# A hybrid encoder layer on one core: one pair's scan a step ahead, some transfers on POOL's queue, values turned later, and a decay product on ScalarE

## The chip, the cores and the metric

The kernel runs on one core of a Trainium2 chip. A core has TensorE (PE, matmuls and 128x128 transposes into PSUM), VectorE (DVE), ScalarE (ACT), GpSimd (POOL) and SyncE (SP, which here only issues transfers). Each engine works through its own list of instructions in order, and waits at an instruction until the data that it needs is there. The metric is the device time of one execution in microseconds (us); three executions are timed, and their median counts.

## The reference

One layer of an encoder trunk over 1024 tokens of width 1024, in float32. Each of three sub-layers is normalised before and after, and added to the residual stream.

```python
h = _rms_norm(x, g_mix_pre[l])
proj = h @ w_in[l]
aq, ak, av, dqkv, dgate, dalpha, dbeta = jnp.split(proj, IN_SPLITS, axis=-1)
...
attn_o = _window_attention(aq, ak, av, attn_sink[l])            # 8 heads of 64, 2 key heads, +-128 tokens
dn_o = _gated_deltanet(dqkv, dgate, dalpha, dbeta, conv_w[l], ...)
mix = jnp.concatenate([attn_o, dn_o], axis=-1) @ w_out[l]
x = x + _rms_norm(mix, g_mix_post[l])
c = _memory_cross_attention(...)                                # 256 memory tokens, 4 heads of 256
x = x + _rms_norm(c, g_cross_post[l])
f = _swiglu(...)                                                # width 2816
x = x + _rms_norm(f, g_ffn_post[l])
```

The gated DeltaNet has four heads, each scanned forwards and backwards over chunks. Within a chunk a triangular system is solved; over the chunks runs

```python
def step(state, inp):
    qg_i, kg_i, u_i, w_i, qk_i, gl_i = inp
    v_new = u_i - jnp.einsum('bhck,bhkv->bhcv', w_i, state)
    o_i = jnp.einsum('bhck,bhkv->bhcv', qg_i, state) + jnp.einsum('bhij,bhjv->bhiv', qk_i, v_new)
    state = state * gl_i[..., None, None] + jnp.einsum('bhck,bhcv->bhkv', kg_i, v_new)
    return state, o_i
```

## The kernel before

Products in full precision are made of three matmuls: each operand is split into its value in the type float32r and the rest (`split`, L99: an ACT copy and a VectorE or POOL subtraction), and high x high, low x high and high x low are summed in PSUM. `gemm_b` (L258) does this over the eight tiles of 128 of the width, 48 matmuls for one projection tile of 128 columns over two halves of 512 tokens.

The kernel hands its instructions to a planner, which keeps the program's order as priority, simulates times, and from these fixes each engine's order, SP's transfers among them. The lists of letters in L36 to L38 give the program's order in three stages:

- `ORDER_1`: projections of the DeltaNet's heads (D), their preparation (P), and the base inverses of two heads together (B, `base_inverse`, L505). A base inverse is a long chain of small VectorE products (L536, L538); that of the second pair of heads still runs while the next stage works.
- `ORDER_2`: `levels` (L, L548) builds the inverses of 128-token chunks from their 32x32 blocks. It fetches blocks with twenty small transfers (L553) into D5, D6, Z0, Z1, of which there is one set, and stores each head's result with four transfers to `d_pz` (L612). `gate_proj` (G), `attn_proj` (A, queries for 0 to 3, keys for 4) and `value_proj` (V) are projections; W stands for two windows of the softmax attention (`next_windows`, L683; a window's scores wait for its queries `qs`, L627).
- `ORDER_3`: M normalises the memory, `s01` makes one step of both scans, W two windows, K one tile of memory keys, V half of the memory values (whose weights are loaded by `load_w`, L127).

`attn_proj` (L723) turns queries and keys by rotary angles: `sn` and `rop` are the projection times sine and cosine (L731, L732), four transfers turn `sn` by 32 partitions into `rot` (L736), and the sum is split into `qhi` and `qlo` and stored to DRAM (L741). `sn`, `rot`, `qhi`, `qlo` and `rop` have two buffers each; `value_proj` (L743) copies its projection to `vT` (L748), which takes a buffer of the tag of `sn`, and PE turns it at once (L751) into `ptv`, split into `vhl`, which the windows use.

`scan(g)` (L773) is a generator for pair `g` of heads, two directions each, so that every tile holds four 128x128 blocks. There are eight steps. A step loads `kv` (k turned, v, k, q; two loads of 512 KB) and `pz` (two of 256 KB) on SP (L795, L796), and yields four times: after R, after the new values (L817), after the new state (L828), after the output. `scan_step` (L943) takes four such pieces, alternating between the pairs it is given. From step 4 on the output is normalised and, one step later, turned, gated and stored by `late` (L867); a ninth call of a scan runs the last `late`. In steps 1 to 3 the output is

```python
nc.vector.tensor_tensor(o, pq, eg(0), ALU.mult)   # L840: query part from PSUM times its decay
nc.vector.tensor_tensor(o, o, po, ALU.add)        # L841
```

and is first read at step 4 or later. The scan's tiles (pool `t3`, L771) take the space of the normalised input `hT` and of the projections' tiles; a tile waits until what lay there has been read.

## Time and profile before

| what | value |
|---|---|
| median of three executions | 1552.57 us (1552.0 to 1556.1) |
| profiled execution, own time | 1553.31 us |
| its span (first to last instruction) | 1551.3 us |
| PE busy | 1493.7 us |
| VectorE busy | 1064.2 us |
| ACT busy | 713.3 us |
| POOL busy | 301.1 us |
| moved by the DMA engines | 247.16 MB, 159 GB/s on average |

The profile is of one execution. Times in it count from the start of its span. "Busy" is the time in which an engine had an instruction in work; a matmul's start and end overlap with its neighbours', so the distance from start to start says more than a duration. The granted clock is the share of TensorE's full rate that the throttle let through. A row of the timeline has the start, the duration, the engine and line, the operation, the tile written and the tiles read, and in brackets how long the engine had stood idle before it and what ended that. "SPq" rows are issues of transfers on SP.

### The profile page before, as it was taken

Reading aid. Unit: us, or ns where it says so; the run is one execution under the profiler, and the core shown is the slowest. Engines: PE = TensorE matmul, PEld = TensorE weight load, DVE = VectorE, ACT = ScalarE, POOL = GpSimd, SP = SyncE. Lnnn points to the kernel's source line nnn. Section 1 sums busy time; section 2 is a strip of 40 time slices with the busy share of each in tenths; the row PEclk is TensorE's granted clock in tenths of the full one; section 3 lists DMA queues with packets and bytes.
Section 4 is the critical chain, followed back from the end, with each engine's and each line's share of the span. In section 5 each row is a group of like instructions: output and inputs, shape, how many; then the busy total and the mean of one; then the engine's idle time right before and its main releaser. Section 6 shows DMA issues by size and latency. Waiting matters only on the chain.

```text
span 1551.3 us, 20930 instructions
## 1 busy us (share of the span) xinstructions
PE 1493.7 (96%) x7451; PEld 1255.3 (81%) x7451; DVE 1064.2 (69%) x1762; ACT 713.3 (46%) x1377; POOL 301.1 (19%) x297
## 2 busy tenths in 40 slices
PE   6999999988999999999999999999999999999998
PEld 5888888777899877888888787888888888888786
DVE  6877898766898765543446377786867654696676
ACT  5665552246556864464335564332323332454532
POOL 2000110000003201163202231443534333000010
PEclk9999999998999999999999999999999999999999
DMA  6244456768988584354223164344433334753355
GB/s 207 73 134 122 133 151 164 214 176 249 328 277 253 169 289 139 127 191 149 69 68 123 55 228 137 116 136 129 142 122 124 102 102 146 288 190 102 109 175 165
DMA packets 267366, 247.16 MB, mean 159 GB/s; under 512 B 39016, under 2 KB 204797, under 8 KB 267261
## 3 DMA queue, kind: packets, MB, share of 16 engines
q1 hardware_dynamic: 267261, 245.82, 50.7%
q8 instruction: 59, 0.97, 0.3%
q14 instruction: 46, 0.38, 0.1%
HBM read 173.65 MB, written 69.50 MB: 157 GB/s over the span
## 4 chain that ended last, share of the span: by engine, by line
PE 77%; DVE 9%; DMA 8%; SPq 2%; ACT 2%; issue 2%; POOL 0%; DVEq 0%; ACTq 0%; POOLq 0%
PE pmg L1020 10%; PE pg L263 10%; PE pE L1208 8%; PE pA L1208 7%; PE pD L1208 7%; PE pcq L263 6%; PE pdX L1398 6%; PE pdA L1398 4%; PE pB L1208 4%; PE psc L787 3%; PE pdX L1491 2%; PE pdD L1398 2%; PE pcs L1112 1%; PE pco L1138 1%; DMA wraw<-in_w_ckv_dram 1%
## 5 line engine op out<-in xcount | busy, mean ns | idle before, releaser
L102 ACT CAST whi<-wraw 128x1024 fp32r<-128x1024 f32 x108 | 113.4, 1050 | 172.9 <-PE pg L263 36.0
L103 DVE TENSOR_TENSOR wlo<-wraw,whi 128x1024 fp32r<-128x1024 f32 x78 | 95.4, 1224 | 69.5 <-ACT whi L102 64.9
L263 PE MATMUL pg<-hhi,whi 128*128 128x512 f32 x352 | 140.5, 400 | 2.0 <-DVE rop L732 2.0
L263 PE MATMUL pg<-hlo,whi 128*128 128x512 f32 x352 | 139.9, 398 | 0.0
L263 PE MATMUL pg<-hhi,wlo 128*128 128x512 f32 x352 | 139.6, 397 | 0.0
L1020 PE MATMUL pmg<-whi,b 128*128 128x512 f32 x384 | 118.3, 394 | 0.4 <-ACT b L102 0.4
L1208 PE MATMUL pA<-s,whi 128*128 128x512 f32 x352 | 109.4, 392 | 1.0 <-ACT m L1225 1.0
L103 POOL TENSOR_TENSOR wlo<-wraw,whi 128x1024 fp32r<-128x1024 f32 x30 | 73.1, 2437 | 142.2 <-ACT whi L102 142.1
L1020 PEld LDWEIGHTS pmg<-whi,b 128*128 128x128 f32 x384 | 71.3, 188 | 15.1 <-ACT b L102 1.3
L263 PEld LDWEIGHTS pg<-hhi,whi 128*128 128x128 f32 x352 | 67.1, 191 | 15.7 <-DVE rop L732 2.4
L263 PEld LDWEIGHTS pg<-hlo,whi 128*128 128x128 f32 x352 | 67.2, 191 | 13.1
L263 PEld LDWEIGHTS pg<-hhi,wlo 128*128 128x128 f32 x352 | 67.0, 190 | 13.1
L1398 PE MATMUL pdX<-dhl,whi 128*128 128x512 f32 x264 | 76.1, 390 | 1.5 <-DVE zv L1453 0.8
L1208 PEld LDWEIGHTS pA<-s,whi 128*128 128x128 f32 x352 | 65.5, 188 | 14.8 <-ACT m L1225 1.5
L1020 PE MATMUL pmg<-wlo,b 128*128 128x512 f32 x192 | 71.5, 392 | 0.0
L1208 PE MATMUL pA<-s,wlo 128*128 128x512 f32 x176 | 68.6, 391 | 0.0
L102 ACT CAST whi<-araw 128x1024 fp32r<-128x1024 f32 (+1 forms) x36 | 35.4, 982 | 71.0 <-PE pdX L1398 27.6
L103 DVE TENSOR_TENSOR wlo<-araw,whi 128x1024 fp32r<-128x1024 f32 (+1 forms) x36 | 40.8, 1133 | 39.5 <-ACT whi L102 39.4
L1285 POOL TENSOR_TENSOR act<-act,up 128x512 f32<-128x512 f32 x33 | 50.1, 1518 | 88.8 <-DVE up L1284 47.3
L288 DVE SCALAR_TENSOR_TENSOR acc<-cp,cols,acc 128x1024 f32<-128x1024 f32 x48 | 61.4, 1281 | 1.5 <-ACT acc L286 0.8
L1398 PEld LDWEIGHTS pdX<-dhl,whi 128*128 128x128 f32 x264 | 49.3, 188 | 12.7 <-issue 1.1
L1258 DVE TENSOR_TENSOR sr<-sr,wraw 128x512 f32<-128x512 f32 x22 | 36.6, 1663 | 28.2 <-POOL sr L1257 28.2
(410 smaller groups left out, 3969.1 us busy)
## 6 DMA issues: line engine op xcount, KB each, us to landing
wraw<-in_w_gate_up_dram SPq DMA_DIRECT2D x52, 512.0 KB, 3.9
kv<-d_kv SPq DMA_DIRECT2D x32, 512.0 KB, 6.7
wraw<-in_w_in_dram SPq DMA_DIRECT2D x22, 512.0 KB, 5.0
b<-in_w_down_dram SPq DMA_DIRECT2D x20, 512.0 KB, 6.9
araw<-d_as SPq DMA_DIRECT2D x20, 512.0 KB, 3.7
pz<-d_pz SPq DMA_DIRECT2D x32, 256.0 KB, 7.1
wraw<-in_w_ckv_dram SPq DMA_DIRECT2D x16, 512.0 KB, 6.4
wraw<-in_w_out_dram SPq DMA_DIRECT2D x16, 512.0 KB, 4.1
```

Source lines behind the costliest of these rows:

```text
L102: nc.scalar.copy(hi, src)
L103: (eng or nc.vector).tensor_tensor(lo, src, f32(hi), ALU.subtract)
L263: nc.tensor.matmul(p_, w[:, k, :], ah[a][:, k, :], start=(k == 0 and i == 0), stop=(k == nk - 1 and i == 2))
L288: nc.vector.scalar_tensor_tensor(acc, cp[:, t:t + S], taps[t], acc, ALU.mult, ALU.add)
L787: nc.tensor.matmul(out[:, d, h, :], lt[:, d, h, :], rt[:, d, h, :], start=True, stop=True)
L1020: nc.tensor.matmul(pp[t], act[a][:, k, tt], w_[:, kk, :], start=(k == 0 and i == 0), stop=(k == KT - 1 and i == 2))
L1112: nc.tensor.matmul(pp[:, t2_, :], q[a][:, ct, tt], kr_[b_][:, ct, :], start=(j == 0 and i == 0), stop=(j == 1 and i == 2))
L1208: nc.tensor.matmul(out_, w[a][:, k, :], xx[b_][:, k, :], start=(start and k == 0 and i == 0), stop=(k == HK - 1 and i == 2), skip_group_ch ...
L1258: nc.vector.tensor_tensor(s[1], s[0], a_[:, 0:HK], ALU.subtract)
L1285: nc.gpsimd.tensor_tensor(o_, o_, up, ALU.mult)
L1398: nc.tensor.matmul(banks[t], a[:, k - k0, tt], w, start=(first and k == 0 and i == 0), stop=(k == NB - 1 and i == 2), skip_group_check=not ...
L1491: nc.tensor.matmul(X[t], a[:, k], w[:, k0 + k], start=False, stop=(k0 + k == NB - 1 and i == 2), skip_group_check=True)
```

## The change

Five edits:

1. The first pair's scan makes its first step before the memory norm M and stays one step ahead; the last of the nine calls is then for the second pair alone.
2. The stores of the inverses (four a head, sixteen in all) are issued from POOL's queue.
3. The loads of a scan's first step (four a pair, eight in all) are issued from POOL's queue.
4. The values are turned in a step of their own, T, behind projection A0. `vT` takes the tag `rot2`, and `rot` lies in the buffer of `qhi`.
5. In steps 1 to 3 the query part is scaled by ACT, four copies of 128x128 with a scale for each partition, where VectorE made one product of 128x512.

```diff
-ORDER_2 = "L0 L1 G0 G1 A4 V A0 A1 L2 L3 W W W A2 A3 G2 G3 W".split()
-ORDER_3 = ("M " + "s01 W K " * 5 + "s01 K " * 3 + "s01 V V").split()
+ORDER_2 = "L0 L1 G0 G1 A4 V A0 T A1 L2 L3 W W W A2 A3 G2 G3 W".split()
+ORDER_3 = ("s0 M " + "s01 W K " * 5 + "s01 K " * 3 + "s1 V V").split()
...
             for d in range(2):
-                nc.sync.dma_start(d_pz[g][d][c4, :, hh, 1].rearrange("c p n -> p c n"), Z[d])
+                nc.gpsimd.dma_start(d_pz[g][d][c4, :, hh, 1].rearrange("c p n -> p c n"), Z[d])
...
             sn = trp.tile([P, HALF], F32, tag="rot", name="sn")
-            rot = trp.tile([P, HALF], F32, tag="rot2", name="rot2")
+            hl = [trp.tile([P, HALF], F32R, tag=t, name=t) for t in ("qhi", "qlo")]
+            rot = f32(hl[0])
...
             nc.vector.tensor_tensor(rop, rop, rot, ALU.add)
-            hl = [trp.tile([P, HALF], F32R, tag=t, name=t) for t in ("qhi", "qlo")]
             split(*hl, rop)
...
+    vTs = []
+
     def value_proj():
 
         pp = proj(w_in[:, 640:768])
         for hf in range(2):
-            vT = trp.tile([P, HALF], F32, tag="rot", name="vT")
+            vT = trp.tile([P, HALF], F32, tag="rot2", name="vT")
             nc.scalar.copy(vT, pp[hf])
+            vTs.append(vT)
+
+    def value_turn():
+
+        for hf in range(2):
             pt = pw.tile([P, 512], F32, tag="pw", name="ptv")
             for j in range(4):
-                nc.tensor.transpose(pt[:, j * P:(j + 1) * P], vT[:, j * P:(j + 1) * P], ident)
+                nc.tensor.transpose(pt[:, j * P:(j + 1) * P], vTs[hf][:, j * P:(j + 1) * P], ident)
...
+            queue = nc.sync if step else nc.gpsimd
             for d in range(2):
-                nc.sync.dma_start(kv[:, d], d_kv[g][cs[d]])
-                nc.sync.dma_start(pz[:, d], d_pz[g][d][cs[d]])
+                queue.dma_start(kv[:, d], d_kv[g][cs[d]])
+                queue.dma_start(pz[:, d], d_pz[g][d][cs[d]])
...
                 mm(pq, kv[:, :, :, 3, :], st)
-                nc.vector.tensor_tensor(o, pq, eg(0), ALU.mult)
+                if half:
+                    for d, h in DH:
+                        nc.scalar.mul(o[:, d, h], pq[:, d, h], EG[:, 0, d, 2 * g + h, step:step + 1])
+                else:
+                    nc.vector.tensor_tensor(o, pq, eg(0), ALU.mult)
                 nc.vector.tensor_tensor(o, o, po, ALU.add)
```

2 lines of the change are left out of this document (1 added, 1 removed).

## The prediction

> **What bounds the kernel now.** First the page: busy time, the DMA queues, the chain that ended last.
>
> ```profile
> PE 1493.7 (96%) x7451; PEld 1255.3 (81%) x7451; DVE 1064.2 (69%) x1762; ACT 713.3 (46%) x1377; POOL 301.1 (19%) x297
> ...
> q1 hardware_dynamic: 267261, 245.82, 50.7%
> ...
> PE 77%; DVE 9%; DMA 8%; SPq 2%; ACT 2%; issue 2%; POOL 0%; DVEq 0%; ACTq 0%; POOLq 0%
> ```
>
> TensorE (PE) is busy for 96% of the span and holds 77% of the chain. The change removes no matmul; it can only remove PE's idle time, and whatever slow matmuls such idle time brings. POOL works 19% of the span and the page lists one data queue, whose issues are all SP's: no transfer from POOL is in this trace.
>
> Second, the stretches in which the edited lines run, by windows (start:end, length, busy us of PE, PEld, DVE, ACT, POOL, granted clock, DMA share, GB/s).
>
> ```profile
> 250.00:260.00 10.00, 7.93 (x48) 6.96 (x46) 8.15 (x20) 3.12 (x9) 0.00 (x0) 0.86 0.57 141
> 260.00:270.00 10.00, 10.00 (x46) 8.34 (x46) 8.90 (x23) 3.59 (x8) 0.00 (x0) 0.80 0.78 219
> ...
> 360.00:370.00 10.00, 9.18 (x56) 8.29 (x55) 5.08 (x18) 6.23 (x15) 0.00 (x0) 0.83 0.28 72
> 370.00:380.00 10.00, 5.58 (x28) 3.99 (x27) 6.73 (x17) 7.88 (x18) 1.59 (x4) 0.83 0.87 245
> ...
> 390.00:400.00 10.00, 7.27 (x49) 5.78 (x47) 7.47 (x22) 5.32 (x12) 0.20 (x1) 1.00 1.09 308
> ...
> 420.00:430.00 10.00, 9.61 (x72) 8.74 (x72) 10.00 (x26) 4.34 (x8) 0.00 (x0) 1.00 1.07 360
> ```
>
> PE idles 2.07 us in the first of these (the value projection), 4.42 at 370 and 2.73 at 390 (the gap between projections and scan). The DMA engines are 0.28 busy at 360 to 370 and full at 390 to 400: the scan's first loads come late and all at once. Third, PE's waits over 250 to 404 us (total, times, longest).
>
> ```profile
> PE pow L666 <- ACT ph L102: 2.4, 1, 2.4
> ...
> PE pck L918 <- ACT whi L102: 1.6, 1, 1.6
> ```
>
> **Part 1, values turned a tile later.** The timeline around the first of these idle times, ACT's row and then PE's:
>
> ```profile
> 256.10 0.58 ACT L748 COPY vT<-pg 128x512 f32<-128x512 f32 x1 [4.30 <-DMA rot<-sn]
> ```
>
> ```profile
> 256.73 0.70 PE L751 MATMUL ptv<-ident,vT 128*128 128x128 f32 x4 [2.07 <-ACT vT L748]
> ...
> 261.50 0.63 PE L263 MATMUL pg<-hhi,whi 128*128 128x512 f32 x1
> 261.93 0.63 PE L263 MATMUL pg<-hlo,whi 128*128 128x512 f32 x1
> ...
> 264.29 0.39 PE L263 MATMUL pg<-hlo,whi 128*128 128x512 f32 x1
> 264.52 0.39 PE L263 MATMUL pg<-hhi,wlo 128*128 128x512 f32 x1
> ```
>
> vT shares its buffers with sn, so ACT stood 4.30 us until sn's rotation had been read, and PE, in order, stood 2.07 behind it. With vT in a tag of its own and the transposes a projection later, both waits go. Worth more than 2.07: matmuls then start 0.43 us apart (261.50 to 261.93) until 264, against 0.23 after (264.29 to 264.52), and the granted clock of the two windows is 0.86 and 0.80. About 7.3 us (256.7 to 264.0) at roughly 57% of the rate lose 3.1 us. Gross 2.07 + 3.1 = 5.2. The Trainium skill ("TensorE: Matmul & The Clock Gate", "Why this matters for your kernels") says that PE falls to the lower clock after idle gaps over some 3 us; by it this gap would cost 2.07 alone, and half of that, 1.0, would stand in the sum. The trace disagrees: 2.07 us idle was followed by 7 us of slow matmuls.
>
> What is late next is the first window:
>
> ```profile
> 312.20 0.55 PE L635 MATMUL psw<-khi,qs 128*128 128x256 f32 x1 [3.56 <-DMA qs<-d_q]
> ```
>
> PE reaches it sooner, but qs hangs on SP's queue and on VectorE's chain of the second base inverse, busy 8.15 and 8.90 of 10 above. If neither moves, the 5.2 is paid back here, unless the planner puts more projection matmuls ahead. Ends 0 and 5.2; I take the middle, 2.6, since SP does move somewhat (part 3).
>
> The turn's buffers: rot now lies in qhi's, so a rotation waits until the store of qhi two halves before has landed, and what is queued behind it on SP (fetches for the levels, weights) waits too; VectorE's rop add waits for the rotation. SP's rows around such a pair,
>
> ```profile
> 264.78 1.09 SPq L741 DMA_DIRECT2D d_k<-qhi  x1
> ...
> 267.80 3.69 SPq L736 DMA_DIRECT2D rot<-sn  x6
> ```
>
> and the stores of the inverses (count, ns least/median/most, first and last start), with the landing of those stores below them:
>
> ```profile
> L612 SPq DMA_DIRECT2D d_pz<-Z x16: 360/532/1554, 272.2 to 373.2; - x16
> DMA to landing us min/median/max: 2.4/4.1/6.0
> ```
>
> The store at 264.78 frees the rotation issued some 4 us later (the second half of the six). A store's landing is taken from L612's, 2.4 to 6.0: up to 2 us of wait, at two tight places. Ends -4 and 0; I take -0.5, nearer the median 4.1.
>
> **Part 2, pair 0's first step ahead, its loads and pair 1's from POOL.**
>
> ```profile
> 359.33 0.40 PE L263 MATMUL pg<-hhi,wlo 128*128 128x512 f32 x1
> ...
> 382.26 1.06 PE L787 MATMUL psc<-kv,pz 128*128 128x128 f32 x4
> 383.11 1.46 PE L903 MATMUL ptm<-ident,mt 128*128 128x128 f32 x10
> ```
>
> SP in the same stretch, ACT's first use of K's weights, and the sizes of the loads (KB each, us to landing):
>
> ```profile
> 363.70 0.55 SPq L761 DMA_DIRECT2D d_gate<-gt  x1
> 369.21 0.94 SPq L612 DMA_DIRECT2D d_pz<-Z  x2
> ...
> 374.47 0.64 SPq L795 DMA_DIRECT2D kv<-d_kv  x1
> ...
> 389.73 0.38 SPq L127 DMA_DIRECT2D wraw<-in_w_ckv_dram  x1
> ```
>
> ```profile
> 398.96 1.04 ACT L102 CAST whi<-wraw 128x1024 fp32r<-128x1024 f32 x1 [3.13 <-DMA wraw<-in_w_ckv_dram]
> ```
>
> ```profile
> kv<-d_kv SPq DMA_DIRECT2D x32, 512.0 KB, 6.7
> ...
> pz<-d_pz SPq DMA_DIRECT2D x32, 256.0 KB, 7.1
> ```
>
> The last projection matmul, the last reader of the space that the scan's tiles take, starts at 359.33, but the first kv load goes out at 374.47: SP stands from 364.3 to 369.2 for the last Z, then issues stores, qs and d_mix. Pair 0's inverses are stored long before. From a queue without those its four loads (two kv, two pz, 1.5 MB) can go some 10 us earlier, into the stretch at a DMA share of 0.28. A step 0 is 12 matmuls at 0.21 us (four from 382.26 to 383.11): 2.55 us of PE work, which can then fill the 4.42 idle at 370, where PE waits on the softmax (pow, 2.4 and others). With up to 3 MB gone from the backlog, the key weights of K, issued at 389.73 and used at 398.96, land earlier, against PE's 1.6 on pck; I take 1.0 of it. Ends 0 (the loads on POOL stay behind Z stores there) and 4.42 + 2.73 = 7.15; taken 2.55 + 1.0 = 3.5. Moving one pair ahead also puts pair 0's later loads and its matmuls a step earlier against W and K, and its last output (four transposes, one DVE product, two stores) out of the tail; total work is the same and PE is at 9.61 of 10 in the row at 420, so 0.
>
> **Part 3, the inverses' stores from POOL.** Sixteen issues of 0.53 median leave SP, 8.5 us in all, and this wait:
>
> ```profile
> SPq L612 <- ACT Z L609: 5.2, 2, 4.8
> ```
>
> PE profits only where it waits for SP: the 3.56 on qs. Of the sixteen, which start at 272.2, only the first head's four stand before that wait: 4 x 0.53 = 2.1 us of SP. Their price on POOL is in no row: the nearest is SP's 0.36 to 1.55, the farthest POOL's longest operation in this stretch:
>
> ```profile
> 242.18 2.25 POOL L530 TENSOR_SCALAR_AFFINE_SELECT A<-A 128x1024 f32<-128x1024 f32 x1 [17.09 <-DVE A L529]
> ```
>
> Ends: a loss (rival C) and 3.56; I take 0.5. The Trainium skill ("DMA: Bandwidth & Descriptors", "Issuing engines are not separate DMA queues") says that issuing from several engines saves only the sequencer's issue time; by it this part and the loads of part 2 would bring less, since 8.5 us of issue time is off PE's path. The trace shows a second saving that the rule does not count, SP's 4.8 us stand in front of one store.
>
> **Part 4, early decay on ACT.** The product that leaves, the nearest kind to what comes, and PE's wait for VectorE in the scan:
>
> ```profile
> L840 DVE TENSOR_TENSOR of<-psc,EG x6: 684/691/692, 415.5 to 452.1; 128x512 f32<-128x512 f32 x6
> ```
>
> ```profile
> L457 ACT ACTIVATE gm<-C,ghi x32: 386/396/479, 73.3 to 208.6; 128x128 fp32r<-128x128 f32 x32
> ```
>
> ```profile
> PE psc L787 <- DVE vg L815: 1.5, 3, 0.8
> ```
>
> Six DVE products leave, 6 x 0.69 = 4.1 us, at a place where DVE is full (10.00 of 10 at 420); 24 scaled copies of the L457 kind come to ACT, 24 x 0.40 = 9.5 us, where ACT is at 4.34 of 10. The result is needed only four steps later, so neither latency counts; what counts is the queue. Ahead of vn or a window's ph stand 1.6 us instead of nothing: at worst 6 x (1.6 - 0.69) = 5.4 us lost; at best PE's 1.5 on vg. I take 0.5, since the full engine is the one relieved.
>
> **Sum.** 2.6 - 0.5 + 3.5 + 0.5 + 0.5 = 6.6 us. The profiled execution took 1553.31 (span 1551.3 and 2.0 around it), 0.74 over the median of 1552.57. 1553.31 - 6.6 = 1546.7, and on the median 1546.0. What a measurement of this kernel can tell from no change is about 0.3%, 4.7 us: under 1547.9 is faster, over 1557.2 slower.
>
> **Rivals.** A, taken back (no change): qs does not come sooner, so part 1 brings 0, and the loads on POOL stay in order behind the last Z stores, which wait for ACT's Z as SP did, so that part 2 fills half a step, 1.3. With the rest as taken (0.5) that is 1.8: 1550.8. For it: L612's 4.8 us wait moves with the store; the planner orders POOL, and the change does not make the loads go first. Against: pair 0 needs nothing from those stores. The change would then not do what it says.
>
> B, more: part 1 whole (5.2), part 2 whole (7.15), the rest 0.5: 12.9, 1539.7. For it: slow matmuls follow the idle at 370 too (clock 0.83), not counted above. Against: PE stays in order behind the same softmax waits.
>
> C, slower: POOL's queue becomes the bound. The buffers of D5, D6, Z are single, so the next head's fetches (L553, on SP) wait until the stores have landed. If a store holds POOL for 2.25 instead of SP's 0.53, four stores delay each of the three changes of head and the scan's loads by 6.9 us; two of these where PE has little other work (the third head to the fourth, and into the scan) are 13.8, less the 6.6: 7.2 slower, 1559.8. It decides from 1.94 us a store: 8 x (1.94 - 0.53) = 11.3 = 6.6 + 4.7. For it: es (L647), on the path of every softmax, queues behind them. Against: POOL has 0.00 to 0.20 busy in most of these windows. The Trainium skill ("SBUF — State Buffer", "SBUF: two separate sides") says that transfers issued from GpSimd have descriptors written over a port that some VectorE operations lock, and gives 0.62 us alone against 3.1 beside such an operation; by that second figure C would decide. No row here shows it.
>
> **How the numbers follow.** Forecast 0.42, A 0.27, B 0.18, C 0.13. Forecast and B are faster: 0.60; A is same: 0.27; C slower: 0.13. The time is the forecast's, 1546.0. The range runs from 1538.0, just past B, to 1557.0, the end of "same", which holds A and the unknown costs of rot (-4) and decay (-5.4): forecast less both is 1554.9. C lies outside, and some 0.05 below.
>
> **What would show it.** Part 1 right: no wait of PE on vT, the windows at 250 and 260 at clock 1.00, and the last projection matmul well before 359. Wrong: a wait on qs longer than 3.56 by what part 1 saved. Part 2 right: kv's first issue, from POOL, before 367, the first psc before 376, PE's idle in the three windows quoted between 360 and 400 under 5 us instead of 8.0 (0.82 + 4.42 + 2.73). Wrong: POOL rows show loads behind Z stores. Part 3: POOL's issues under 1.9 us each, and no longer wait of SP's L553 on d_pz. Part 4: DVE under 10 at the third step, ACT up by about 9 us, no wait of PE on vn. A PE chain over 400 to 540 longer than before, or a gain lost after 540, would make the whole sum wrong.

## The result, and the profile after

The changed kernel takes 1559.66 us in the median of five executions (1557.87 to 1562.86), the kernel before 1552.57 in the median of five on the same chip: a ratio of 1.0036 with a 95% interval of 1.0019 to 1.0053. By the ratio that is 5.6 us slower (the two medians are 7.1 apart), where 6.6 us faster was predicted, and 1559.66 is above the range's end of 1557.0. The profiled execution took 1559.66, its span 1558.0.

The page after, the same rows as shown of before; no matmul has gone, ACT is busy 5.4 us more and POOL 16.5, in 24 instructions more each:

```profile
PE 1491.0 (96%) x7451; PEld 1250.1 (80%) x7451; DVE 1059.4 (68%) x1756; ACT 718.7 (46%) x1401; POOL 317.6 (20%) x321
```

The windows after (start:end, length, busy us of PE, PEld, DVE, ACT, POOL, granted clock, DMA share, GB/s):

```profile
250.00:260.00 10.00, 10.00 (x59) 8.72 (x59) 8.29 (x19) 2.79 (x9) 0.00 (x0) 1.00 0.57 148
260.00:270.00 10.00, 8.45 (x55) 7.27 (x54) 9.57 (x26) 2.60 (x6) 0.00 (x0) 1.00 0.71 189
360.00:370.00 10.00, 7.85 (x57) 6.87 (x56) 6.26 (x18) 6.83 (x16) 5.33 (x9) 1.00 0.61 182
370.00:380.00 10.00, 6.18 (x24) 4.45 (x24) 5.87 (x18) 7.22 (x20) 3.91 (x10) 0.83 1.01 354
380.00:390.00 10.00, 7.80 (x37) 6.53 (x38) 7.75 (x20) 1.23 (x4) 0.20 (x1) 0.83 1.06 375
390.00:400.00 10.00, 7.42 (x49) 6.17 (x48) 7.67 (x21) 8.66 (x23) 0.00 (x0) 0.97 0.93 271
...
420.00:430.00 10.00, 9.22 (x79) 9.00 (x79) 8.53 (x26) 6.58 (x21) 0.20 (x1) 1.00 1.00 271
```

The first two rows are as foretold: 114 matmuls where there were 94, at full clock. Those from 360 to 400 are not. PE idles 8.6 us in the three windows at 360, 370 and 390 (8.0 before; under 5 was the mark) and 2.2 at 380 (0.35 before). The DMA engines were to be relieved there; they are full 10 us earlier (1.01 at 370 where it was 0.87), and ACT, at 1.23 of 10, stands.

What PE reaches when (timeline; start, duration):

```profile
356.55 0.39 PE L263 MATMUL pg<-hhi,wlo 128*128 128x512 f32 x1
...
377.25 0.61 PE L794 MATMUL psc<-kv,pz 128*128 128x128 f32 x4
...
386.12 1.06 PE L794 MATMUL psc<-kv,pz 128*128 128x128 f32 x4
...
391.36 1.16 PE L794 MATMUL psc<-vn,pz 128*128 128x128 f32 x8 [1.04 <-ACT vn L825]
392.35 1.04 PE L915 MATMUL ptm<-ident,mt 128*128 128x128 f32 x8
```

The last projection ends 2.8 us earlier than before and the first scan matmul comes 5.0 earlier. But the scan's first product (8 of the trace's matmuls) stands half done from 377.9 to 386.1, and M's transposes come at 392.35 where they came at 381.41. V, the memory values, starts 7.2 us later than before (538.2 against 531.0), and the end is 6.7 later. So the early stage won about 5 us, and the stretch from 377 to 540 lost 12.

### The profile page after: what moved, and what is told of

Its sections match the earlier page's. It is cut to its first block, busy times and chain, and to the rows that moved or that the text cites. A ratio compares the mean times of both kernels' runs of the same rounds, so it can differ in the third digit from the quotient of the medians.

```text
span 1558.0 us, 20995 instructions
## 1 busy us (share of the span) xinstructions
PE 1491.0 (96%) x7451; PEld 1250.1 (80%) x7451; DVE 1059.4 (68%) x1756; ACT 718.7 (46%) x1401; POOL 317.6 (20%) x321
```

## The experiments

Each ratio is to the kernel before on the same chip. The kernel before spread from 1548.0 to 1559.1 over all its executions, so a single profiled execution shows where things happen, while differences of some us in the total are read from the ratios. The table gives the ratio (interval) and, from the profiled execution, the start of the last levels' matmul, the first scan load's issue, the start of VectorE's first product in the scan (vg), and the start of V (us).

The places scatter too. The traces of before, decay_only, before_ao_gt and decay_ao_gt list the same instructions in the same order on every engine up to some 408 us, and yet their levels end anywhere from 369.1 to 373.6. In the changed kernel, no_decay, after_ao and no_decay_ao_gt PE's order is the same up to some 408 us: 364.9 to 369.3. So a difference under some 4.5 us in one of these columns says little, while the time from the load to vg differs by 1.2 and 0.7 us within these two groups.

| kernel | edits | ratio | levels | load | vg | V |
|---|---|---|---|---|---|---|
| before | none | 1 | 370.5 | 374.5 | 387.4 | 531.0 |
| changed | 1-5 | 1.0036 (1.0019-1.0053) | 364.9 | 367.9 | 387.2 | 538.2 |
| skew_only | 1 | 1.0009 (0.9994-1.0024) | 368.4 | 372.3 | 381.8 | 529.7 |
| queues_only | 2, 3 | 1.0000 (0.9989-1.0011) | 365.4 | 368.7 | 391.9 | 529.2 |
| values_only | 4 | 1.0055 (1.0036-1.0074) | 373.9 | 377.9 | 390.1 | 533.3 |
| decay_only | 5 | 1.0034 (1.0019-1.0049) | 369.4 | 373.3 | 386.7 | 530.5 |
| no_skew | 2-5 | 1.0044 (1.0029-1.0059) | 366.5 | 369.4 | 393.3 | 534.5 |
| no_decay | 1-4 | 1.0028 (1.0019-1.0037) | 366.2 | 369.2 | 388.4 | 538.1 |
| alias_only | rot of 4 | 1.0011 (1.0003-1.0020) | 371.2 | 375.2 | 387.2 | 530.4 |
| vt_now | 4, turned at once | 1.0076 (1.0064-1.0088) | 380.3 | 384.8 | 397.5 | 542.1 |
| values_gt | 4 + gt | 0.9997 (0.9984-1.0011) | 371.3 | 375.3 | 387.3 | 531.5 |
| vt_now_gt | vt_now + gt | 1.0035 (1.0019-1.0052) | 372.7 | 376.7 | 389.1 | 532.0 |
| after_ao | 1-5 + ao | 1.0012 (1.0000-1.0025) | 369.3 | 372.5 | 392.4 | 539.5 |
| no_decay_ao_gt | 1-4 + ao, gt | 1.0006 (0.9996-1.0017) | 365.9 | 369.2 | 388.9 | 534.8 |
| before_ao_gt | ao, gt | 0.9998 (0.9983-1.0012) | 369.1 | 373.1 | 385.3 | 529.7 |
| decay_ao_gt | 5 + ao, gt | 1.0025 (1.0013-1.0038) | 373.6 | 378.0 | 391.2 | 534.3 |
| loads_sp | 1, 2, 4, 5 | 0.9988 (0.9974-1.0003) | 366.1 | 369.0 | 379.5 | 529.0 |
| e124 | 1, 2, 4 | 0.9992 (0.9980-1.0005) | 363.1 | 365.9 | 376.3 | 526.7 |
| rest_sp | 1, 2, 4 + ao, gt | 0.9995 (0.9982-1.0009) | 365.2 | 368.0 | 378.4 | 530.2 |
| loads01_pool | 1-5, step 1 too | 1.0091 (1.0069-1.0113) | 367.2 | 370.2 | 383.7 | 547.0 |

### The edits one by one

After the result the first theory was S: the pair that is ahead of M delays M and the memory keys, whose matmuls fill PE during the scan. Its rivals were D, the copies of the decay in ACT's order, and Q, loads that stand behind the last stores on POOL.

no_skew, the changed kernel with edit 1 undone:

```diff
-ORDER_3 = ("s0 M " + "s01 W K " * 5 + "s01 K " * 3 + "s1 V V").split()
+ORDER_3 = ("M " + "s01 W K " * 5 + "s01 K " * 3 + "s01 V V").split()
```

> The changed kernel with edit 1 undone (M first, both pairs in step, nine calls as before); edits 2 to 5 stay. Theory S (skew): the order with pair 0 ahead of M costs the 11 to 12 us by which the scan stretch fell behind, because M and the first memory keys, whose matmuls fill PE between the dependent products of the scan, come some 10 us later and pair 0's step-1 loads crowd the stretch from 367 to 400; then this kernel keeps the 5 us won before 370 and loses nothing after: about 1548. Rival D (decay): ACT, in order, stands with the 24 copies in front of vn and the windows' exponentials; then undoing the skew changes little: 1557 to 1560. Rival Q (queue): the loads behind the last stores of the inverses on POOL hold up the first step; then also about 1557 to 1560, and its first psc is late as well.

Measured 1.0044: theory S falls as the whole cause, with the skew away nothing is won.

skew_only, the kernel before with edit 1:

```diff
-ORDER_3 = ("M " + "s01 W K " * 5 + "s01 K " * 3 + "s01 V V").split()
+ORDER_3 = ("s0 M " + "s01 W K " * 5 + "s01 K " * 3 + "s1 V V").split()
```

> The kernel before with edit 1 alone. Theory S: 8 to 12 us slower than before, 1561 to 1564, with the transposes of M at 390 or later instead of 381.4 and the first K weights issued at 395 or later instead of 389.7. Rivals D and Q: within 2 us of before, 1551 to 1555, since neither ACT nor POOL has been given anything.

Measured 1.0009, no difference; from the load to vg it takes 9.5 us where it took 12.9, and M's transposes come at 384.9, 3.5 us later than before. S falls here too.

decay_only, the kernel before with edit 5:

```diff
-                nc.vector.tensor_tensor(o, pq, eg(0), ALU.mult)
+                if half:
+                    for d, h in DH:
+                        nc.scalar.mul(o[:, d, h], pq[:, d, h], EG[:, 0, d, 2 * g + h, step:step + 1])
+                else:
+                    nc.vector.tensor_tensor(o, pq, eg(0), ALU.mult)
```

> The kernel before with edit 5 alone. Rival D: 4 to 8 us slower than before, 1557 to 1561, with waits of PE on vg, vn and ph between 400 and 540 longer by as much. Theory S and rival Q: within 2 us of before (the working put it at -0.5), 1551 to 1554.

Measured 1.0034, 5.3 us: in D's range. But PE's waits on vg, ph and pl from 400 to 540 sum to 3.9 us in its profiled execution against 3.0 before, so the loss is not seen at the place that D names. That execution is the fastest of its twelve, 4.5 us under their median, so it need not show the loss at all.

values_only, the kernel before with edit 4 (its lines stand in the change's diff):

```diff
-ORDER_2 = "L0 L1 G0 G1 A4 V A0 A1 L2 L3 W W W A2 A3 G2 G3 W".split()
+ORDER_2 = "L0 L1 G0 G1 A4 V A0 T A1 L2 L3 W W W A2 A3 G2 G3 W".split()
...
-            rot = trp.tile([P, HALF], F32, tag="rot2", name="rot2")
+            rot = f32(hl[0])
...
-            vT = trp.tile([P, HALF], F32, tag="rot", name="vT")
+            vT = trp.tile([P, HALF], F32, tag="rot2", name="vT")
```

> The kernel before with edit 4 alone (values turned a tile later, new places for vT and rot). By the working: 2.6 less 0.5 faster, 1550.5; if the 5.2 us of idle time and slow matmuls are kept whole, 1547.5; if rotations that now wait for a store of qhi cost what they could, 1554. Theories S, D and Q all leave this kernel at 1547 to 1551; if it is slower than before, none of them is the whole cause.

Measured 1.0055, 8.6 us slower, where every theory had it faster. None of them is the whole cause.

queues_only, the kernel before with edits 2 and 3:

```diff
-                nc.sync.dma_start(d_pz[g][d][c4, :, hh, 1].rearrange("c p n -> p c n"), Z[d])
+                nc.gpsimd.dma_start(d_pz[g][d][c4, :, hh, 1].rearrange("c p n -> p c n"), Z[d])
...
+            queue = nc.sync if step else nc.gpsimd
```

> The kernel before with edits 2 and 3: stores of the inverses and the loads of the scan's first steps from POOL's queue; nothing else. The three edits measured alone add up to 1.0009 x 1.0034 x 1.0055 = 1.0098 of before, and all five measured 1.0036. If the effects of the edits add, these two have to bring 0.6%: 0.993 to 0.996 of before, about 1546. Theory P (planner): the effects don't add, because each edit makes the planner lay out the whole stretch from 250 to 570 us anew, and what comes of it scatters by some 0.3 to 0.5% either way; then this kernel may come out anywhere from 0.997 to 1.005. By the working (0.5 for the stores, and the loads' share of the 3.5) it is 1 to 4 us faster, 1551 to 1554.

Measured 1.0000. The effects do not add: alone the edits make 1.0009 x 1.0000 x 1.0055 x 1.0034 = 1.0098, together 1.0036.

no_decay, the changed kernel with edit 5 undone (the diff of decay_only, reversed):

```diff
-                        nc.scalar.mul(o[:, d, h], pq[:, d, h], EG[:, 0, d, 2 * g + h, step:step + 1])
+                nc.vector.tensor_tensor(o, pq, eg(0), ALU.mult)
```

> The changed kernel with edit 5 undone (the early decay by VectorE as before); edits 1 to 4 stay. Edit 5 alone measured 1.0034 of before (5 us slower). Theory D (decay): the 24 copies stand on ACT in front of vn and the windows' exponentials, in this kernel as in that: 4 to 6 us faster than the changed kernel, 1.000 to 1.001 of before, with ACT's wait of 7.5 us at ao kept, but no waits of PE on ph and vg above those of before between 400 and 540 us. Rival P: edit 5 shifted the planner's order and not ACT's load; then within 2 us of the changed kernel or slower than it, 1.003 to 1.006.

Measured 1.0028, within the interval of the changed kernel; V still starts 7.1 us late. The decay is not what delays the scan.

### Where edit 4 loses

Theory R was that the rotation in qhi's buffer holds up SP; rival O, that the turn's new place costs.

alias_only, the rotation alone:

```diff
-            rot = trp.tile([P, HALF], F32, tag="rot2", name="rot2")
+            hl = [trp.tile([P, HALF], F32R, tag=t, name=t) for t in ("qhi", "qlo")]
+            rot = f32(hl[0])
```

> The kernel before with one line of edit 4 alone: rot lies in the buffer of qhi; the values stay in the tag of sn and are turned at once. Edit 4 alone measured 8 us slower (1.0055 of before) where the working had it 2.1 faster. Theory R (rot): a rotation that has to wait until the store of qhi two halves before has landed holds SP, and with it the first windows' queries and the fetches of the levels; then this kernel keeps most of that loss: 1.003 to 1.006 of before, 1559 to 1564. Rival O (order): the loss of edit 4 comes from the turn's new place and from the different order that the planner makes around it; then this kernel is within 0.2% of before, 1552 to 1558 beside a median of 1555.

Measured 1.0011, 1.7 us (0.5 to 3.1): a small part. R falls as the main cause.

vt_now, edit 4 with the turn directly behind V:

```diff
-ORDER_2 = "L0 L1 G0 G1 A4 V A0 T A1 L2 L3 W W W A2 A3 G2 G3 W".split()
+ORDER_2 = "L0 L1 G0 G1 A4 V T A0 A1 L2 L3 W W W A2 A3 G2 G3 W".split()
```

> The kernel before with edit 4, but with T directly behind V, so that the values are turned at once; vT in its own buffers and rot in those of qhi as in edit 4. Theory R: as slow as edit 4 alone, 1.004 to 1.007 of before. Rival O, if the turn's new place is what costs: faster than edit 4 alone by 4 us or more, 1.000 to 1.002 of before, and PE's wait on vT shorter than the 2.07 us of before, as only ACT's copy is left in it.

Measured 1.0076, the slowest so far, though its last value transpose comes 13.9 us earlier than before (251.6 against 265.5). Both theories miss. In both kernels the first window's matmul stays where it was (312.5 and 312.3 against 312.2), and the last levels come later. Part of this is PE's clock: in vt_now's trace the granted clock is 0.50 from 368.8 to 385.6, with PE busy for 16.0 of these 16.8 us, some 8 us of work lost (an estimate, half of 16.0). Another part shows in ACT's and SP's rows of edit 4 alone:

```profile
346.03 0.60 ACT L767 ACTIVATE gt<-pg 128x512 f32<-128x512 f32 x1
...
359.93 1.28 ACT L767 ACT_TABLE_LOAD   x1 [3.26 <-DMA d_gate<-gt]
...
366.52 0.60 ACT L767 ACTIVATE gt<-pg 128x512 f32<-128x512 f32 x1 [3.40 <-DMA d_gate<-gt]
367.02 0.27 ACT L598 ACTIVATE z<-ps 128x128 f32<-128x128 f32 x1
```

```profile
347.01 4.22 SPq L612 DMA_DIRECT2D d_pz<-Z  x4
351.32 2.83 SPq L553 DMA_DIRECT2D D<-d_inv  x4
...
356.07 0.46 SPq L768 DMA_DIRECT2D d_gate<-gt  x1
356.57 5.59 SPq L553 DMA_DIRECT2D Z<-d_inv  x8
```

The gate tiles gt have two buffers. The first is written at 346.03, but its store goes out at 356.07, behind the inverses' stores and fetches in SP's list. ACT stands 3.26 and then 3.40 us for buffers, and z of the last levels, next in its list, comes at 367.02. Before, that store went out at 346.42, ACT stood 3.82 us once, at 352.54, and z came at 361.59.

This was theory W: ACT's wait for a store's buffer holds up what stands behind it. The rival P was that the planner's new order scatters the time by itself. The test gives gt four buffers:

```diff
-            gt = trp.tile([P, HALF], F32, tag="rop", name="gt")
+            gt = trp.tile([P, HALF], F32, tag=("rop", "rot2")[h % 2], name="gt")
```

values_gt, edit 4 with that line:

> Edit 4 alone (1.0055 of before), with one thing more: the gate tiles gt of one head take the tag of vT, of the other the tag of rop, so that the four have four buffers. Edit 4 alone had ACT waiting 3.4 and 3.3 us for the store of an earlier gt at 359 to 366 us, with the last head's levels behind it, and those levels ended 3.4 us later than before (373.9 against 370.5). Theory W: with those waits gone the levels end at 367 to 371 and the loss shrinks by 3 to 7 us: 1.001 to 1.0035 of before. Rival P: the levels end no earlier than 373, and the kernel stays at 1.0045 to 1.0065.

Measured 0.9997: the whole loss is gone, and ACT's rows have no wait on d_gate left:

```profile
363.92 0.60 ACT L767 ACTIVATE gt<-pg 128x512 f32<-128x512 f32 x1
364.41 0.27 ACT L598 ACTIVATE z<-ps 128x128 f32<-128x128 f32 x1
```

W is borne out: the two kernels list the same instructions in the same order on PE, VectorE and POOL from first to last, so P's scatter of PE's order is not what was lost. It is more than W foretold (1.001 to 1.0035), and only 2.6 us of it stand at the levels (371.3 against 373.9). The clock goes along with it: over its executions it averages 0.9849 in edit 4 alone and 0.9881 here, which at most is 0.0032 of 1555 us or 5.0 of the 9.0 us between the two (an estimate from the means). The 2.1 us of gain that the working had (2.6 less 0.5) do not show either: the first window waits 3.1 us for qs and starts at 314.4.

vt_now_gt, the turn at once with that line:

```diff
-ORDER_2 = "L0 L1 G0 G1 A4 V A0 A1 L2 L3 W W W A2 A3 G2 G3 W".split()
+ORDER_2 = "L0 L1 G0 G1 A4 V T A0 A1 L2 L3 W W W A2 A3 G2 G3 W".split()
...
-            gt = trp.tile([P, HALF], F32, tag="rop", name="gt")
+            gt = trp.tile([P, HALF], F32, tag=("rop", "rot2")[h % 2], name="gt")
```

> Edit 4 with the values turned at once (1.0076 of before, the slowest so far), with gt in four buffers added. Theory W (ACT's wait for gt's buffer holds up the last levels): most of the loss goes, 0.9995 to 1.003 of before, and the last levels end before 373 us instead of 380.3. Rival P (the planner's order): 1.005 to 1.008, levels at 377 or later.

Measured 1.0035, half of 1.0076; the levels end at 372.7 instead of 380.3. The levels are where W has them, but in the fastest of twelve executions, 6.9 us under their median, and beside a trace with 16.8 us at half clock, so W can't claim the whole 7.6. The ratio misses W's upper end narrowly: some 0.35% of this order has another cause that no run settles.

### ACT at ao

The same wait stands in the changed kernel at the windows' result ao, which has one buffer. ACT's rows of the changed kernel:

```profile
390.11 0.58 ACT L669 COPY ao<-pow 64x512 f32<-64x512 f32 x1 [7.49 <-DMA d_mix<-ao]
390.72 0.58 ACT L825 COPY vn<-psc 128x512 f32<-128x512 f32 x1
```

The addition lets ao take the two halves of its place in turn:

```diff
-        ao = tw.tile([P, 4, P], F32, tag="ao", name="ao", bufs=1)[0:64]
-        nc.scalar.copy(ao, po[64:128])
-        nc.vector.tensor_tensor(ao, po[0:64], ao, ALU.add)
+        a, b = (slice(64 * i, 64 * i + 64) for i in (n % 2, 1 - n % 2))
+        ao = aos[a]
+        nc.scalar.copy(ao, po[b])
+        nc.vector.tensor_tensor(ao, po[a], ao, ALU.add)
```

after_ao, the changed kernel with it:

> The changed kernel, with one thing more: the windows' result ao, which has one buffer of 64 partitions, takes the upper and the lower 64 partitions of its place in turn, so that ACT needn't wait until the store of the window before has landed. In the changed kernel ACT stood 7.49 us at one ao and 3.0 at another (0.61 and 2.9 in the kernel before), with vn of pair 0's first step and the windows' ph behind it. Theory W (buffers): this wait is where the scan fell behind; then the wait is gone, vn comes some 7 us earlier, the transposes of M come at 385 to 388 instead of 392.4, and the kernel is 5 to 8 us faster than the changed one: 0.998 to 1.0005 of before, where the changed one is 1.0036. Rival P (planner and DMA): the DMA engines are full from 370 to 400 us whatever ACT does, so the wait moves to the next load: 1.002 to 1.005 of before.

Measured 1.0012, 0.24% less than the changed kernel (give or take 0.21, the two intervals' halves combined as a root of squares). The time is nearer W than P, but the place is not as W has it: M's transposes come at 395.5, and vg itself only at 392.4, still 19.9 us after the first load. The wait was real, and something else delays the first step.

no_decay_ao_gt, edits 1 to 4 with both additions:

```diff
+            gt = trp.tile([P, HALF], F32, tag=("rop", "rot2")[h % 2], name="gt")
...
+        ao = aos[a]
```

> Edits 1 to 4 (without the early decay on ACT) and both additions. Edits 1 to 4 alone are 1.0028 of before, with 8.2 us of ACT's waits at ao. Theory W: those waits go, and the gain that the first 370 us had kept (levels 4 to 5 us earlier) is kept to the end: 0.996 to 0.9985 of before, 1548 to 1552, faster than both kernels. Rival P: 1.001 to 1.004.

Measured 1.0006 against 1.0028 without the additions: again less, by 0.22% (give or take 0.14). W's 0.996 to 0.9985 is missed; the gain before 370 is still lost after it.

before_ao_gt, the control, both additions and no edit:

```diff
+            gt = trp.tile([P, HALF], F32, tag=("rop", "rot2")[h % 2], name="gt")
...
+        ao = aos[a]
```

> The kernel before with both additions (ao in turn in two halves, gt in four buffers) and none of the five edits: the control for the two runs beside it. It has ACT's waits too, 3.8 us at gt and 3.5 at ao. Theory W: 0 to 4 us faster than before, 0.9975 to 1.0; how much says what the additions bring by themselves. Rival P: within 0.3% either way.

Measured 0.9998: the additions bring nothing by themselves. What they bring beside the edits, they take from what the edits had made late.

### Two queues

The first loads' landing is what is left. The scan loads of the changed kernel between 364 and 392 us, then of the kernel before (count, ns least/median/most, first and last start; us from issue to landing):

```profile
L803 POOL DMA_DIRECT2D kv<-d_kv x4: 533/533/565, 367.9 to 371.1; - x4
L803 SPq DMA_DIRECT2D kv<-d_kv x4: 451/535/666, 369.4 to 373.4; - x4
DMA to landing us min/median/max: 6.9/11.0/13.9
```

```profile
L795 SPq DMA_DIRECT2D kv<-d_kv x8: 319/376/867, 374.5 to 385.8; - x8
DMA to landing us min/median/max: 5.4/7.0/7.8
```

Before, SP sent the loads in the order of their use, and a load landed after 7.0 us. Changed, the first step's loads go out from POOL while SP, with nothing in front, sends the second step's at the same time, and they land after 11.0. Theory Q2 says that the two queues share the DMA engines, so that the later loads hold up the first. The rival S is again the pair that is ahead.

loads_sp, the changed kernel with edit 3 undone:

```diff
-            queue = nc.sync if step else nc.gpsimd
             for d in range(2):
-                queue.dma_start(kv[:, d], d_kv[g][cs[d]])
-                queue.dma_start(pz[:, d], d_pz[g][d][cs[d]])
+                nc.sync.dma_start(kv[:, d], d_kv[g][cs[d]])
+                nc.sync.dma_start(pz[:, d], d_pz[g][d][cs[d]])
```

> The changed kernel with edit 3 undone: the loads of the scan's first step go out from SP again, in order ahead of those of the second; edits 1, 2, 4, 5 stay. In the changed kernel the first steps' loads from POOL's queue and the second steps' from SP's went out together (367.9 to 373.5 us), and a load took 11.0 us in the median to land, 13.9 at most, where SP's queue alone had 7.0 and 7.8; the first step's vg came at 387.2 although its loads had gone out 6.6 us earlier than before. Theory Q2 (the two queues share the DMA engines, so that later loads hold up the first): landings of 7 to 8 us again, vg at 381 to 384, M's transposes at 385 to 388, and the kernel 3 to 6 us faster than the changed one: 0.9995 to 1.0015 of before. Rival S (pair 0 ahead of M costs it, whatever the queue): M's transposes at 391 or later, 1.003 to 1.005.

Measured 0.9988, 0.48% less than the changed kernel (give or take 0.22). Its scan loads, its PE rows and ACT:

```profile
L802 SPq DMA_DIRECT2D kv<-d_kv x10: 319/412/1442, 369.0 to 386.1; - x10
DMA to landing us min/median/max: 6.1/8.0/9.3
```

```profile
381.00 1.07 PE L794 MATMUL psc<-vg,kv 128*128 128x128 f32 x8
382.62 1.16 PE L794 MATMUL psc<-vn,pz 128*128 128x128 f32 x8 [0.55 <-ACT vn L824]
383.62 1.69 PE L914 MATMUL ptm<-ident,mt 128*128 128x128 f32 x14
```

The first load goes out 1.1 us later than in the changed kernel, vg comes 7.7 us earlier and M's transposes 8.7. ACT's wait at ao is gone without the addition. Every sign moves Q2's way, and beyond its ranges (vg at 381 to 384, 0.9995 to 1.0015). S is not borne out. Edit 3 costs, beside the other edits.

Q2's reason is borne out only in part. The last of the first step's four loads, pz, in the changed kernel and in loads_sp:

```profile
L804 POOL DMA_DIRECT2D pz<-d_pz x2: 536/552/569, 368.5 to 369.5; - x2
DMA to landing us min/median/max: 7.1/8.4/9.7
```

```profile
L803 SPq DMA_DIRECT2D pz<-d_pz x2: 432/690/949, 370.5 to 372.0; - x2
DMA to landing us min/median/max: 5.5/5.9/6.2
```

The four took 6.9 to 9.7 us to land beside SP's loads, 5.5 to 6.4 with all loads on SP. But as they went out earlier, the last of them landed at 379.25 in the changed kernel and at 378.2 in loads_sp: 1.1 us apart, where vg is 7.7 apart. The difference is in PE's list. PE's rows in the changed kernel, and the second half of the first product in loads_sp:

```profile
380.10 0.50 PE L666 MATMUL pow<-ph,vhl 128*128 128x512 f32 x1 [2.24 <-ACT ph L102]
...
384.95 0.50 PE L666 MATMUL pow<-pl,vhl 128*128 128x512 f32 x1 [1.77 <-DVE pl L103]
```

```profile
378.31 1.19 PE L794 MATMUL psc<-kv,pz 128*128 128x128 f32 x4 [0.15 <-DMA pz<-d_pz]
```

In loads_sp PE takes the second half as soon as it has landed. In the changed kernel the planner has put window products in front of it, which wait for ACT and VectorE, and the second half runs at 386.12, 6.9 us after its data was there. It is the same wherever edits 1 and 3 stand together with the second step's loads on SP: the changed kernel, no_decay, after_ao and no_decay_ao_gt, which share one order of PE there, run that half 6.9 to 8.1 us after its data and need 19.2 to 19.9 us from the first load to vg. The four kernels with edit 1 and all loads on SP (skew_only, loads_sp, e124, rest_sp; the last three share an order) run it 0.1 to 0.5 us after its data and need 9.5 to 10.5. So most of what the second queue cost the first step is the place that its product got in PE's order, and one or two us are the landings. Why the planner chose that place is not on record.

Behind vg two things follow in the changed kernel: ACT's vn stands behind ao (until 390.72), and M's transposes stand behind vn's product. With M in front (queues_only) vg is as late, at 391.9, but M's transposes come at 383.9, and nothing is lost. no_skew has M in front too, at 384.9, and still measures 1.0044; what it loses, beside edits 4 and 5, this account doesn't cover.

loads01_pool, the changed kernel with both steps' loads on POOL:

```diff
-            queue = nc.sync if step else nc.gpsimd
+            queue = nc.sync if step > 1 else nc.gpsimd
```

> The changed kernel with the loads of the second step on POOL's queue as well, behind those of the first; all else as changed. Theory Q2 (two queues share the DMA engines): first and second step stand in one order again, the first step's loads land in 9 us at most, its vg comes at 380 to 384 us instead of 387.2, M's transposes at 388 or earlier, and the kernel gains 3 us or more on the changed one: 1.0015 of before or less. Rival (POOL's queue is slow for these loads): landings of 10 us and more stay, vg at 386 or later, 1.003 to 1.007 of before.

Measured 1.0091. The landings are between (kv's: 9.1 in the median, 10.4 at most, where Q2 has 9 at most) and vg comes at 383.7, where Q2 has it: the first four loads take 6.7 to 8.3 us, and the second half of the first product runs 2.7 us after its data. So loads from POOL do not by themselves make the first step late. The time is far off both, for another reason. ACT's, DVE's and PE's rows:

```profile
396.45 0.58 ACT L669 COPY ao<-pow 64x512 f32<-64x512 f32 x1 [8.87 <-DMA d_mix<-ao]
```

```profile
397.07 0.68 DVE L670 TENSOR_TENSOR ao<-pow,ao 64x512 f32<-64x512 f32 x1 [8.51 <-ACT ao L669]
...
398.40 1.42 DVE L908 TENSOR_SCALAR mt<-mt,mrs 128x1024 f32<-128x1024 f32 x2
```

```profile
399.21 1.11 PE L915 MATMUL ptm<-ident,mt 128*128 128x128 f32 x4 [10.57 <-DVE mt L908]
```

Read upwards: PE waits 10.57 us for the scaled memory mt, which stands in DVE's list behind ao, which waits for ACT's ao, which waits for the store of the window before. It is theory W's wait again, now on PE's path. Its store went out among the loads, at 382.4. For the question of the queues only the landings and vg of this run count.

### The decay once more, and what is left

decay_ao_gt, edit 5 with both additions:

```diff
+                        nc.scalar.mul(o[:, d, h], pq[:, d, h], EG[:, 0, d, 2 * g + h, step:step + 1])
...
+        ao = aos[a]
```

> The kernel before with edit 5 (decay by ACT) and both additions (ao in two halves, gt in four buffers); the additions alone measured 0.9998 of before, edit 5 alone 1.0034. Theory W: edit 5's loss is ACT standing for ao's buffer, 6.6 us in its trace against 3.5 before; then 0.999 to 1.001. Theory D (ACT's own work in front of vn and ph): 1.0025 to 1.0045, with waits of PE on vg, vn and ph between 400 and 540 us longer than before.

Measured 1.0025: at the low end of D, above W. In its profiled execution, the slowest of twelve, the levels already end 4.5 us later than in the control (373.6 against 369.1), though all engines have the same order there and the first scaled copy comes only at 416.2. That difference is scatter between executions, and the trace settles neither theory. What the record does show is the clock: over the executions it averages 0.9858, against 0.9885 in the kernel before on the same chip. That is at most 0.0027 of 1554 us, 4.2 us, as much as the whole 3.9; for edit 5 alone it is 0.9870 against 0.9885, at most 2.3 of the 5.3 us (estimates from the means). Why PE should have a lower clock with this edit is not shown.

e124, edits 1, 2 and 4:

```diff
-                        nc.scalar.mul(o[:, d, h], pq[:, d, h], EG[:, 0, d, 2 * g + h, step:step + 1])
+                nc.vector.tensor_tensor(o, pq, eg(0), ALU.mult)
...
-            queue = nc.sync if step else nc.gpsimd
```

> Edits 1, 2 and 4 alone: the first steps' loads on SP, the decay on VectorE as before, neither addition. With the decay on ACT this kernel measured 0.9988 of before. Theory D (ACT's copies cost about 0.3% wherever they stand): 0.995 to 0.997, about 1547 to 1549. Rival (the decay costs only where PE has no other work, and the effects don't add): 0.998 to 1.0005.

Measured 0.9992, with the decay on ACT 0.9988: beside these edits the decay costs nothing that can be measured. Why it costs 0.3% alone stays open.

rest_sp, the same with both additions:

```diff
+            gt = trp.tile([P, HALF], F32, tag=("rop", "rot2")[h % 2], name="gt")
...
+        ao = aos[a]
```

> Edits 1, 2 and 4 with both additions; the first steps' loads on SP and the decay on VectorE as before. If theories W and Q2 name the causes, the gain before 370 us (levels 4 to 5 us earlier with the stores on POOL) reaches the end: 0.996 to 0.9985 of before, 1549 to 1552. If something after it takes the gain back whatever starts earlier (the rate of the DMA engines in the scan, the softmax's chain): 0.9995 to 1.0015.

Measured 0.9995. The three kernels without edit 3 beat the changed one by 0.4 to 0.5%, and none is distinguishable from the kernel before. The gain before 370 us (levels 4 to 7 us earlier) does not reach the end in full. e124 is 4.3 us ahead at V and 1.4 in its span; whether the rest is lost at a place or in the spread of single executions is open.

## Why the prediction was wrong

**Part 1, values (2.6 foretold).** The mechanism at 250 to 270 us was right: in the changed kernel no wait on vT, clock 1.00, and the last transposes 4.7 us earlier (260.8 against 265.5); in edit 4 alone 4.2 earlier, with the clock at 0.83 in the second window. Two things failed. "What is late next is the first window": with edit 4 alone everything was paid back there, since qs did not move (the wait grew from 3.56 to 4.82, and psw started at 312.5); of the ends 0 and 5.2 the lower held, which is rival A's. With edit 2 beside it, psw of the changed kernel did come 2.2 us earlier, at 309.98. And the chain was not followed past that window. With the order shifted, gt's store fell behind SP's other work, ACT stood 6.7 us for its buffer, and the kernel lost 8.6: a term that the sum did not have. The rotation in qhi's buffer, foretold at 0.5 of loss within 0 to 4, measured 1.7. A smaller slip: the granted clock was 0.50 from 257.25 to 264.0, so the slow matmuls cost some 3.4 us, half of that stretch, not 3.1 at "57% of the rate".

**Part 2, loads from POOL (3.5 foretold).** The loads did stand behind the last Z stores there (367.14, then 367.91), the sign that was named as wrong; the first psc came at 377.25, not before 376, and PE's idle time was 8.6, not under 5. The step that failed is that the work of a step 0 "can then fill the 4.42 idle at 370". The data was there, 3.3 us earlier than before (379.25 against 382.5), but half of the first product stood behind window products in PE's order until 386.12, and vg came at 387.22 where it came at 387.39. That work was also counted too small: 12 products are 24 matmuls in the trace (8 each that read kv and pz, vg, vn), 5.1 us at the 0.21 that was taken, more than the gap. The second step that failed is "with up to 3 MB gone from the backlog": a queue is not a set of engines, and nothing left the backlog (DMA share 1.01 and 1.06 in the windows at 370 and 380, 0.87 and 1.03 before). K's weights went out at 396.09 instead of 389.73, and K's first matmul came at 409.4 instead of 400.1. The Trainium skill ("DMA: Bandwidth & Descriptors", "Issuing engines are not separate DMA queues") says that transfers started by different engines end on the same 16 DMA engines and interleave there. The traces agree: the first step's loads took 6.9 to 9.7 us beside SP's and 5.4 to 6.4 before. "Total work is the same, so 0" failed too: M, which now stands behind that first step, came 11 us later, and PE's busy time in 400 to 540 fell from 135.58 to 131.47. With edit 3 undone the kernel is 0.48% faster and ends level with the kernel before.

**Part 3, stores from POOL (0.5 foretold).** The price is settled:

```profile
L612 POOL DMA_DIRECT2D d_pz<-Z x16: 750/750/978, 272.6 to 367.1; - x16
...
DMA to landing us min/median/max: 2.8/4.9/7.4
```

A store holds POOL for 0.75 us, far under the 1.94 from which rival C decides. The effect was undersized in place: with edits 2 and 3 alone the levels end 5.1 us earlier than before, 3.7 earlier than the earliest of the four executions with before's order. The sign that SP's L553 would no longer wait on d_pz did not come: 2.6 us between 250 and 380, where it was 1.6. And it hides part of edit 4's loss: with SP's list shorter, ACT waits 1.5 us for gt in the changed kernel instead of 6.7. That is one reason why the effects don't add.

**Part 4, decay (0.5 foretold).** The counts were right (24 copies of 0.37 us, DVE at 8.53 instead of 10.00 in the window at 420). PE's wait on vn came, but at 391 us, before any scaled copy, behind ao. Alone the edit lost 5.3 us, by the low end of -5.4; with edits 1, 2 and 4 it lost nothing. (With both losses at their ends the working's 1554.9 should be 1555.4: -0.5 to -4 and 0.5 to -5.4 are 9.4 us off the forecast.)

**The rivals.** The time is close to rival C's 1559.8 by luck: POOL's issues are short, and what made the first step late is its place in PE's order, with ACT standing at ao behind it. A had two of the signs (qs unmoved with edit 4 alone, loads behind the stores), but ended at no change. B's larger gain is nowhere. No rival had the first step's place in PE's order, or ACT standing for a store's buffer.

## What to carry to other kernels

Data that lands earlier is worth something only if its consumer's place in its own engine's order moves too. So compare the time of landing with the time of first use before calling a load late: here 6.9 us lay between them. A second queue frees urgent loads from what stood in front, and frees what stood behind to be in flight with them: ask which transfers will then go out together. Where an engine fills a tile that a store must empty, follow that store in its queue, since work that comes earlier on PE is worth nothing when the next engine in the chain stands for a buffer. And measure edits within the whole as well as alone: a planner lays out what follows each of them anew, and two kernels that share an order up to a point are, up to there, two executions of the same thing.

## What the runs showed of the hardware

A short idle time of PE was again followed by slow matmuls. The changed kernel's timeline:

```profile
298.49 1.97 PE L587 MATMUL ps<-mov,L 128*128 128x64 f32 x16 [2.30 <-DVE mov L605]
...
300.68 0.63 PE L263 MATMUL pg<-hhi,whi 128*128 128x512 f32 x1
301.10 0.63 PE L263 MATMUL pg<-hlo,whi 128*128 128x512 f32 x1
...
304.45 0.40 PE L263 MATMUL pg<-hlo,whi 128*128 128x512 f32 x1
304.69 0.39 PE L263 MATMUL pg<-hhi,wlo 128*128 128x512 f32 x1
```

After 2.30 us of idle time the matmuls start 0.42 us apart until 304 and 0.24 after. The Trainium skill ("TensorE: Matmul & The Clock Gate", "Why this matters for your kernels") puts the gap that costs the clock at some 3 us; here a shorter one was enough, a second time.

But the length of the gap is not what decides here. The granted clock of these traces is 1.00 or 0.50, and the stretches at 0.50 are pieces of some 3.4 us or several of them in a row. Windows of that length of the changed kernel:

```profile
368.70:372.10 3.40, 0.95 (x4) 0.53 (x4) 1.13 (x3) 3.40 (x10) 2.96 (x6) 1.00 1.00 240
372.12:375.50 3.38, 3.19 (x10) 2.45 (x9) 3.35 (x11) 2.07 (x5) 0.99 (x3) 0.50 0.96 340
...
378.96:382.36 3.40, 2.04 (x10) 1.44 (x10) 2.28 (x5) 1.98 (x6) 0.00 (x0) 1.00 1.03 402
382.38:385.76 3.38, 1.51 (x7) 0.95 (x6) 3.01 (x9) 0.24 (x1) 0.00 (x0) 1.00 1.03 397
385.80:389.20 3.40, 3.40 (x16) 3.30 (x16) 2.43 (x7) 0.00 (x0) 0.20 (x1) 0.50 1.06 366
```

PE was busy for 0.95 of 3.40 us, and the next window ran at half clock; the same after 1.51 of 3.38. The idle 2.24 us that ended at 380.10 lay across two windows, busy 2.03 and 2.04 of 3.40, and cost no clock. Over the twenty traces, between 60 and 1540 us and cut into windows of 3.41 us in step with their half-clock pieces, all 68 at full clock in which PE was busy under 0.4 of the time were followed by half clock, 53 of 376 between 0.4 and 0.8, and none of 7972 above. So the same gap can cost 1.7 us more (an estimate, half of a piece of 3.4) or nothing, by where it falls, which is one source of the scatter between executions: in each of the five sets of executions of the kernel before that were run beside the experiments, the slower ones have the lower clock (correlations of -0.5 to -0.8).
